# A four-tap convolution whose first tap is written by ScalarE instead of VectorE, in a one-layer hybrid decoder step

## The chip, the cores and the metric

The kernel runs on one core of a Trainium2 chip. The core has TensorE (PE in the profile; its weight loads are listed as PEld), VectorE (DVE), ScalarE (ACT), GpSimd (POOL) and SyncE (SP, which here only issues DMAs). Each engine works through its own instructions strictly in the order of its queue. The metric is the device time of one execution in microseconds (us).

## What is computed

One step of a decoder layer with three parallel branches: differential attention, a Mamba-2 state space branch (SSD) and a gated delta rule branch (GDN). One input projection feeds all of them. The columns of the projection that go to the SSD (1024) and to the GDN (1536) pass through a causal convolution of four taps per channel before their SiLU; the query, key, value and gate columns do not.

```python
proj = jnp.dot(h, w['in'])                     # 1024 prompt rows, 8 sample rows

def causal_conv(x, buf, w):                    # CONV_W = 4
    L = x.shape[1]
    xp = jnp.concatenate([buf.astype(x.dtype), x], axis=1)
    y = xp[:, 0:L] * w[0]
    for i in range(1, CONV_W):
        y = y + xp[:, i:i + L] * w[i]
    return y, xp[:, L:]

xbc, conv1 = causal_conv(xbc, conv0, conv_w)   # SSD: silu(xbc + conv_b)
qkv, conv1 = causal_conv(qkv, conv0, conv_w)   # GDN: silu(qkv)
```

## The kernel before

The input projection is computed feature-major. An item is 128 output columns (channels, on the partitions); there are 44 items: 4 query, 4 key, 4 value, 12 gate (`z_item`), 8 SSD convolution (`x_item`) and 12 GDN convolution (`g_item`) items. `proj_fm` takes the items in a fixed list. An item is three blocks of 344 token columns, n = 0, 1, 2. A block is 24 matmuls (8 slices of the contraction, times three products of high and low halves of the operands, line 458) into one PSUM bank of the ring `pj`, which has three banks; so the matmuls of a block can't begin before the bank of the block three places earlier has been read out. When a block is done, the item's `sink` reads the bank. Query, key, value and gate items are read by one ScalarE copy per block (lines 563, 577, 600, 990). Convolution items are read by `conv_item`'s sink on VectorE: one `tensor_scalar_mul` with the factor of the last tap (line 964), and then three `scalar_tensor_tensor` instructions (helper `stt`, line 167) that read the bank shifted by one to three columns and add onto `y` (tile `cy`, 128 x 1024 in SBUF). After the third block the item's `tail` columns are copied (line 971), and `silu_flush` runs SiLU over whole `cy` tiles on ScalarE, with loads of the activation table when the function changes (lines 155, 186). The convolution has 20 items, so 60 blocks, 60 first taps and 180 further taps.

ScalarE also splits the weights of the next item: `w_split` writes the high half (`whi`, line 155 through `act`), and GpSimd the low half (`wlo`, line 201). There are three buffers for half an item's weights.

Other streams run beside the projection. `gdn_head` inverts a triangular matrix of each GDN head: its blocks go from tile `LT` to DRAM (`invd`, line 1126) and come back as `Dm` (line 1129); VectorE does 31 elimination steps of two instructions on tile `U` with `Dm` (lines 1141 and 1142, helper `tt` at line 159); `U` goes to DRAM (line 1146) and comes back into `LT` (line 1149); then TensorE transposes it (line 1158), and the head's recurrence follows. All four of these DMAs are issued from ScalarE's queue, so what stands behind one of them there waits until its condition holds. `sample_attention` streams cache pages: GpSimd multiplies key pages (`kt`, line 840), VectorE reduces them to `lg` (line 841), TensorE multiplies value pages (`vt`, line 886).

The order on each engine is laid down when the kernel is built: a scheduler places the instructions of all streams by its own estimate of when they can run, with the priorities that `drive` and `boost` give. On the chip the queues then run in that order.

Of the kernel before, what the change touches and what calls it, by code (L numbers as in the profile page):

```python
# [13 lines left out]
AF = mybir.ActivationFunctionType  # L14
# [73 lines left out]
def trunk_kernel(  # L88
# [9 lines left out]
    V, S, G, TE, SP = nc.vector, nc.scalar, nc.gpsimd, nc.tensor, nc.sync  # L98
# [37 lines left out]
    def unit(shape, dt=F32, n="u"):  # L136
        return up.tile(shape, dt, tag="u", name=nm(n))
# [15 lines left out]
    def act(out, in_, func, bias=0.0, scale=1.0, accum=None):  # L153
        if accum is None:
            return S.activation(out, in_, func, bias=bias, scale=scale)  # L155
        return S.activation(out, in_, func, bias=bias, scale=scale, accum_out=accum)  # L156
# [9 lines left out]
    def stt(out, a, s, b, op0, op1):  # L166
        return V.scalar_tensor_tensor(out=out, in0=a, scalar=s, in1=b, op0=op0, op1=op1)  # L167
# [777 lines left out]
    def silu_flush():  # L945
        for y, bias, done in late_silu:
            i = act(y, y, AF.Silu, bias=bias)
        exp_ln_tables(i)
        for y, bias, done in late_silu:
            done(y)  # L950
        late_silu.clear()

    def conv_item(c0, wb, ws, ti, tj, done, flush, silu_bias=0.0):
        wv = [vec[:, wb + i * ws + ti:wb + i * ws + ti + 1] for i in range(4)]
        cur = [None]

        def sink(n, ps):
            if n == 0:
                cur[0] = unit([P, T], n="cy")
            y = cur[0]  # L960
            o = 3 if n else 0
            m = CH if n < 2 else CH - NS
            c0_ = n * CH
            V.tensor_scalar_mul(y[:, c0_:c0_ + m], ps[:, o:o + m], wv[3])
            for i in range(3):
                s_ = 0 if n else 3 - i
                q = o - 3 + i + s_
                yv = y[:, c0_ + s_:c0_ + m]
                stt(yv, ps[:, q:q + m - s_], wv[i], yv, ALU.mult, ALU.add)
            if n == 2:  # L970
                V.tensor_copy(tail[:, tj, :], ps[:, o + m - 3:o + m + NS])
                late_silu.append((y, silu_bias, done))
                if flush:
                    silu_flush()

        return (c0, sink, 3)
# [623 lines left out]
    def pages_of(f):  # L1600
        return take(smp, f * S_ALL), f * S_ALL
# [89 lines left out]
    for n1 in CUTS:  # L1691
# [5 lines left out]
        ps = pages_of(SF[1] * f)  # L1697
# [239 lines left out]
```

## Time and profile before

| | us |
|---|---|
| median of 3 runs | 1262.76 |
| lowest, highest run | 1250.82, 1265.09 |
| the profiled execution | 1275.71 |
| its span, first to last instruction | 1274.0 |
| TensorE busy in the span | 1139.0 |
| VectorE, ScalarE, GpSimd busy | 803.8, 476.2, 641.8 |

The profiled execution took 1.7 us more than its span, and 13 us more than the median run. The projection lies between about 60 and 856 us of the span. Then come the rest of the attention, of the SSD and of the GDN, and from about 1120 us the output projection.

Busy time is the time in which an engine executes something. A row of a view in order of time has the start, the duration, the engine, the line, the operation, output<-input by the tiles' names, the shape and the number of merged instructions; in square brackets stands the idle time of the engine just before, and what ended it. PEclk is the granted clock of TensorE, as a share of its upper level.

### The profile page before, as it was taken

How to read it: one execution, taken by the hardware profiler on the slowest of the kernel's cores; microseconds unless marked ns; L12 is line 12 of the kernel's file. 1: busy time of each engine (PE TensorE's matmuls, PEld its weight loads, DVE VectorE, ACT ScalarE, POOL GpSimd, SP SyncE). 2: the span in 40 equal slices, each digit the busy share in tenths (PEclk: the TensorE clock that was granted, in tenths of full speed). 3: DMA queues.
4: the chain of work that ended last, by engine and by line, in shares of the span. 5: the costliest groups of instructions: out<-in, count | busy, mean ns of one | idle time of the engine just before them, and what ended most of it. 6: DMA issues, size and time to landing. Idle time of an engine off the chain costs nothing.

```text
span 1274.0 us, 22286 instructions
## 1 busy us (share of the span) xinstructions
PE 1139.0 (89%) x7364; PEld 956.3 (75%) x7365; DVE 803.8 (63%) x1933; ACT 476.2 (37%) x1014; POOL 641.8 (50%) x778
## 2 busy tenths in 40 slices
PE   5999998988889988989997899978898999799997
PEld 4799887777658868768876779856577778678876
DVE  6613386538658668944655924877877888664444
ACT  6332223201123532233352244345647658341111
POOL 3747964644567573473975688841032151241100
PEclk9999998988879998998998999999998999899999
DMA  8646864993796883695896799998884663961420
GB/s 297 199 164 206 275 206 126 339 317 92 233 315 202 279 278 84 219 323 182 281 338 189 220 333 319 332 266 222 243 201 126 160 172 114 297 216 54 130 69 34
DMA packets 246451, 275.56 MB, mean 216 GB/s; under 512 B 31905, under 2 KB 163376, under 8 KB 246322
## 3 DMA queue, kind: packets, MB, share of 16 engines
q1 hardware_dynamic: 168082, 214.44, 52.1%
q10 hardware_dynamic: 78256, 59.72, 16.7%
q8 instruction: 58, 0.95, 0.3%
q14 instruction: 55, 0.45, 0.1%
HBM read 231.59 MB, written 42.67 MB: 215 GB/s over the span
## 4 chain that ended last, share of the span: by engine, by line
PE 49%; DMA 18%; DVE 17%; ACT 4%; issue 4%; POOL 3%; SPq 3%; ACTq 1%; DVEq 0%; POOLq 0%
PE b L458 20%; PE b L1826 10%; DVE U L159 4%; DMA vt<-in_cache_v_dram 4%; PE pv L886 3%; DMA kt<-in_cache_k_dram 2%; DMA w<-in_w_in_dram 2%; POOL kt L840 2%; DVE lg L841 2%; DVE cy L167 2%; SPq L821 1%; PE b L745 1%; DMA sbc<-bcd 1%; DVE e L721 1%; DMA Dm<-invd 1%
## 5 line engine op out<-in xcount | busy, mean ns | idle before, releaser
L458 PE MATMUL b<-hh,whi 128*128 128x344 f32 (+1 forms) x2016 | 504.6, 333 | 25.5 <-DVE cy L167 13.9
L840 POOL TENSOR_TENSOR kt<-kt,qb 128x256 f32<-128x256 f32 x512 | 364.1, 747 | 137.8 <-DMA kt<-in_cache_k_dram 82.4
L458 PEld LDWEIGHTS b<-hh,whi 128*128 128x128 f32 x2016 | 358.0, 194 | 57.1 <-issue 30.3
L458 PE MATMUL b<-hh,wlo 128*128 128x344 f32 (+1 forms) x1008 | 329.1, 331 | 3.4 <-POOL wlo L201 3.3
L841 DVE TENSOR_REDUCE lg<-kt 128x16 f32<-128x1024 f32 x128 | 154.8, 1212 | 101.8 <-POOL kt L840 94.7
L458 PEld LDWEIGHTS b<-hh,wlo 128*128 128x128 f32 x1008 | 194.5, 194 | 16.2 <-issue 10.9
L201 POOL TENSOR_TENSOR wlo<-w,whi 128x512 fp32r<-128x512 f32 x86 | 111.0, 1295 | 96.7 <-ACT whi L155 95.4
L1826 PE MATMUL b<-wo,mh 128*128 128x512 f32 (+1 forms) x408 | 121.8, 380 | 0.0
L155 ACT ACTIVATE whi<-w 128x512 fp32r<-128x512 f32 x86 | 53.8, 630 | 141.2 <-PE b L458 86.2
L167 DVE SCALAR_TENSOR_TENSOR cy<-b,vec,cy 128x341 f32<-128x341 f32 (+4 forms) x180 | 98.9, 564 | 1.5
L886 PE MATMUL pv<-vt,wz 128*32 128x512 f32 x512 | 78.8, 631 | 16.2 <-DMA vt<-in_cache_v_dram 12.7
L1826 PEld LDWEIGHTS b<-wo,mh 128*128 128x128 f32 x408 | 74.7, 188 | 14.1
L1826 PE MATMUL b<-wo,ml 128*128 128x512 f32 (+1 forms) x204 | 77.2, 378 | 0.0
L1794 POOL TENSOR_TENSOR ml<-zt,mh 128x512 fp32r<-128x512 f32 x16 | 22.4, 1401 | 104.6 <-ACT mh L1793 89.5
L155 ACT ACT_TABLE_LOAD x36 | 46.2, 1283 | 30.4 <-DMA qh<-qfd 11.0
L159 DVE TENSOR_TENSOR U<-U,Dm 128x60 f32<-128x60 f32 (+24 forms) x124 | 42.3, 341 | 16.7 <-DMA Dm<-invd 14.7
L156 ACT ACTIVATE e<-e,nmx 128x128 f32<-128x128 f32 (+7 forms) x64 | 49.1, 768 | 8.5 <-issue 5.2
L718 PE MATMUL b<-kTh,qh 128*128 128x128 f32 (+3 forms) x96 | 40.9, 433 | 9.4 <-DVE mx L721 7.2
L159 DVE TENSOR_TENSOR U<-U 128x60 f32<-128x60 f32 (+24 forms) x124 | 44.4, 358 | 2.4
L159 DVE TENSOR_TENSOR y<-b,gate 128x512 f32<-128x512 f32 (+1 forms) x17 | 11.1, 659 | 53.6 <-PE b L1826 53.6
L721 DVE CUSTOM_DVE_ANT_0 e<-b,bt 128x512 f32<-128x512 f32 (+3 forms) x64 | 36.9, 581 | 12.0 <-PE b L719 9.9
L1826 PEld LDWEIGHTS b<-wo,ml 128*128 128x128 f32 x204 | 38.4, 188 | 7.3
(524 smaller groups left out, 1964.0 us busy)
## 6 DMA issues: line engine op xcount, KB each, us to landing
kt<-in_cache_k_dram SPq DMA_DIRECT2D x256, 256.0 KB
vt<-in_cache_v_dram SPq DMA_DIRECT2D x256, 256.0 KB
w<-in_w_in_dram ACTq DMA_DIRECT2D x82, 256.0 KB
zfd<-zf ACTq DMA_DIRECT2D x12, 512.0 KB
wo<-in_w_out_dram SPq DMA_DIRECT2D x12, 512.0 KB
om<-mixd SPq DMA_DIRECT2D x24, 256.0 KB
xt<-in_x_prompt_dram SPq DMA_DIRECT2D x8, 512.0 KB
hx<-in_w_ada_dram SPq DMA_DIRECT2D x16, 256.0 KB
```

The costliest lines, as they stand in the source:

```text
L155: return S.activation(out, in_, func, bias=bias, scale=scale)
L156: return S.activation(out, in_, func, bias=bias, scale=scale, accum_out=accum)
L159: return V.tensor_tensor(out=out, in0=a, in1=b, op=op)
L167: return V.scalar_tensor_tensor(out=out, in0=a, scalar=s, in1=b, op0=op0, op1=op1)
L201: G.tensor_tensor(out=lo, in0=w32, in1=hi.bitcast(F32), op=ALU.subtract)
L458: TE.matmul(ps[:, 0:N], a, b[k][:, sl], start=(i == 0), stop=(i == 23))
L718: TE.matmul(ps[:, 0:b - a], qh[:, m, ts], kT[m][:, a:b], start=True, stop=False)
L721: V.tensor_tensor_reduce(out=e[m][:, a:b], in0=ps[:, 0:b - a], in1=bias, scale=1.0, scalar=-3.0e38, op0=ALU.add, op1=ALU.max, accum_out=mx ...
L840: G.tensor_tensor(out=kt[:, j, c], in0=kt[:, j, c], in1=qb[:, c], op=ALU.mult)
L841: V.tensor_reduce(out=lg[:, 2 * g:2 * g + 2, :], in_=kt.rearrange("p j (a d) -> p j a d", d=64), axis=AX.X, op=ALU.add)
L886: mm = TE.matmul(pv[32 * r:32 * r + 32, :], wz[:, 2 * g + j, :], vt[:, j, :], start=(b == 0 and g < 2), stop=(b == NS - 1 and g >= 14 and ...
L1826: TE.matmul(ps[c], m[a][:, kt % 4, :], w[kt][:, c[0]:c[1]], start=(kt == KT[0] and i == 0), stop=(kt == KT[-1] and i == 2))
```

## The change

One line of `conv_item`'s sink: the first tap of a convolution block is no longer a VectorE multiplication but a ScalarE activation `Copy` whose scale is the same per-channel factor. The three further taps, the copy of the tail and all else stay in the code as they were.

```diff
             m = CH if n < 2 else CH - NS
             c0_ = n * CH
-            V.tensor_scalar_mul(y[:, c0_:c0_ + m], ps[:, o:o + m], wv[3])
+            act(y[:, c0_:c0_ + m], ps[:, o:o + m], AF.Copy, scale=wv[3])
             for i in range(3):
                 s_ = 0 if n else 3 - i
```

Sixty instructions leave VectorE's queue and sixty stand on ScalarE's. Since the scheduler places all streams anew, other instructions change their places too, on all engines; ScalarE's queue has 58 table loads where it had 53.

The first place is VectorE in the elimination steps of the first GDN head. `cy_3400` is a convolution item and `b_3375` the bank of its first block. Before:

```order
L159 TENSOR_TENSOR U_2827<-U_2827,Dm_2822 128x65
L964 TENSOR_SCALAR cy_3400<-b_3375,vec 128x344
L159 TENSOR_TENSOR U_2827<-U_2827 128x5x13
L159 TENSOR_TENSOR kb_3417<-kN_2484,f_340_2569 128x1024
L167 SCALAR_TENSOR_TENSOR cy_3400<-b_3375,vec,cy_3400 128x341
L159 TENSOR_TENSOR U_2827<-U_2827,Dm_2822 128x60
L159 TENSOR_TENSOR lg_2030<-lg_2030,b_3182 128x264
L167 SCALAR_TENSOR_TENSOR cy_3400<-b_3375,vec,cy_3400 128x342
L159 TENSOR_TENSOR U_2827<-U_2827 128x5x12
L964 TENSOR_SCALAR cy_3400<-b_3428,vec 128x344
L167 SCALAR_TENSOR_TENSOR cy_3400<-b_3375,vec,cy_3400 128x343
```

After the change, on the same engine:

```order
L159 TENSOR_TENSOR U_2827<-U_2827,Dm_2822 128x76
L159 TENSOR_TENSOR kb_3417<-kN_2484,f_340_2569 128x1024
L159 TENSOR_TENSOR U_2827<-U_2827 128x4x19
L167 SCALAR_TENSOR_TENSOR cy_3400<-b_3375,vec,cy_3400 128x341
L159 TENSOR_TENSOR U_2827<-U_2827,Dm_2822 128x72
L167 SCALAR_TENSOR_TENSOR cy_3400<-b_3375,vec,cy_3400 128x342
L159 TENSOR_TENSOR U_2827<-U_2827 128x4x18
L167 SCALAR_TENSOR_TENSOR cy_3400<-b_3375,vec,cy_3400 128x343
L159 TENSOR_TENSOR U_2827<-U_2827,Dm_2822 128x68
```

The three taps that empty bank `b_3375` now stand some nine elimination steps earlier (the steps count down from 128x76 over 128x72 and 128x75 to 128x60).

The second place is ScalarE at the end of the elimination of the second GDN head (`U_5170`). `cy_5812` is a convolution item, `cy_6109` the next one (with banks `b_6084` and then `b_6149`). Before:

```order
L155 ACTIVATE whi_5949<-w_734_5785 128x512
L155 ACTIVATE whi_6114<-w_764_6080 128x512
L194 DMA w_765_6082<-in_w_in_dram 128x4x128
L155 ACTIVATE cy_5812<-cy_5812,vec 128x1024
L186 ACT_TABLE_LOAD
L194 DMA w_786_6267<-in_w_in_dram 128x4x128
L1146 DMA invd<-U_5170 256x1x32 x4
L1582 DMA yxd<-cy_5812 128x1024
L1149 DMA LT_4934<-invd 32x8x32 x4
L155 ACTIVATE whi_6178<-w_765_6082 128x512
```

After:

```order
L155 ACTIVATE whi_5949<-w_734_5785 128x512
L1146 DMA invd<-U_5170 256x1x32 x4
L155 ACTIVATE cy_5812<-b_5985,vec 128x336
L194 DMA w_765_6082<-in_w_in_dram 128x4x128
L155 ACTIVATE whi_6114<-w_764_6080 128x512
L1149 DMA LT_4934<-invd 32x8x32 x4
L155 ACTIVATE cy_5812<-cy_5812,vec 128x1024
L186 ACT_TABLE_LOAD
L155 ACTIVATE cy_6109<-b_6084,vec 128x344
L194 DMA w_786_6267<-in_w_in_dram 128x4x128
L1582 DMA yxd<-cy_5812 128x1024
L155 ACTIVATE cy_6109<-b_6149,vec 128x344
```

The first taps of three blocks now stand behind the store of `U` (line 1146) or behind the load that waits for that store to land (line 1149), where before no read-out of a bank stood. On TensorE, the transposes of this head (line 1158) have moved too: they stood inside block `b_6271`, the first block of the item behind `cy_6109`, with 15 of its 24 matmuls and 12 of the next block ahead of them; now they stand inside block `b_6202`, the last block of `cy_6109`, with eight of its matmuls behind them.

## Rows read from the trace of the kernel before

**Rows 1.** Stretch, length; busy (count) of PE, PEld, DVE, ACT, POOL; PEclk, DMA, GB/s.
```profile
60.00:856.00 796.00, 720.92 (x4663) 615.82 (x4661) 483.54 (x974) 249.12 (x430) 517.95 (x649) 0.95 0.76 244
```

**Rows 2.** The page: busy time by engine; the chain that ended last, by engine.
```profile
PE 1139.0 (89%) x7364; PEld 956.3 (75%) x7365; DVE 803.8 (63%) x1933; ACT 476.2 (37%) x1014; POOL 641.8 (50%) x778
...
PE 49%; DMA 18%; DVE 17%; ACT 4%; issue 4%; POOL 3%; SPq 3%; ACTq 1%; DVEq 0%; POOLq 0%
```

**Rows 3.** The chain between 60 and 856 us, shares by line.
```profile
by line: PE b L458 31.5%; DVE U L159 6.7%; DMA vt<-in_cache_v_dram 4.8%; PE pv L886 4.3%; issue 4.2%; DMA kt<-in_cache_k_dram 3.5%; POOL kt L840 3.0%; DVE lg L841 2.9%; DVE cy L167 2.9%; DMA w<-in_w_in_dram 2.5%; SPq L821 1.8%; DMA sbc<-bcd
```

**Rows 4.** Groups by shape: count, busy us, mean ns, idle us before, releasers.
```profile
L155 ACT ACT_TABLE_LOAD x36 | 46.2, 1283 | 30.4 <-DMA qh<-qfd 11.0 <-DMA vt<-in_cache_v_dram 4.8 <-DMA LT<-invd 3.5
...
L964 DVE TENSOR_SCALAR cy<-b,vec 128x344 f32<-128x344 f32 x40 | 22.4, 567 | 3.8 <-PE b L458 3.8
...
L155 ACT ACTIVATE em<-b,bs 128x256 f32<-128x256 f32 x32 | 13.5, 473 | 24.6 <-PE b L1110 17.1 <-DMA vt<-in_cache_v_dram 4.8 <-PE b L458 2.6
...
L964 DVE TENSOR_SCALAR cy<-b,vec 128x336 f32<-128x336 f32 x20 | 11.1, 555 | 7.0 <-PE b L458 7.0
...
L990 ACT COPY zf<-b 128x344 f32<-128x344 f32 x24 | 10.4, 447 | 49.1 <-PE b L458 21.3 <-DMA invd<-U 10.8 <-DMA vt<-in_cache_v_dram 8.0
L155 ACT ACTIVATE oC<-b,f 128x128 f32<-128x128 f32 x28 | 10.2, 364 | 50.7 <-DVE vn L159 42.2 <-DVE lg L841 6.4 <-POOL wlo L201 2.2
```

**Rows 5.** Line 167 on the convolution's tile: count, shortest/median/longest ns, first and last start.
```profile
L167 DVE SCALAR_TENSOR_TENSOR cy<-b,vec,cy x180: 546/565/577, 163.0 to 850.1; 128x344 f32<-128x344 f32 x60, 128x336 f32<-128x336 f32 x60, 128x341 f32<-128x341 f32 x20, 128x342 f32<-128x342 f32 x20
```

**Rows 6.** TensorE's waits, 160 to 856 us: us in total, times, longest.
```profile
PE b L458 <- DVE cy L167: 13.9, 8, 5.3
...
PE b L458 <- ACT zf L990: 5.8, 1, 5.8
...
PE b L608 <- ACT vT L600: 5.2, 1, 5.2
PE b L458 <- DVE tail L971: 4.3, 1, 4.3
```

**Rows 7.** VectorE in order of time, first head's elimination.
```profile
295.06 1.22 DVE L159 TENSOR_TENSOR U<-U,Dm 128x72 f32<-128x72 f32 x1
...
302.25 0.57 DVE L964 TENSOR_SCALAR cy<-b,vec 128x344 f32<-128x344 f32 x1
...
307.77 0.56 DVE L167 SCALAR_TENSOR_TENSOR cy<-b,vec,cy 128x343 f32<-128x343 f32 x1
...
327.91 0.56 DVE L964 TENSOR_SCALAR cy<-b,vec 128x336 f32<-128x336 f32 x1
...
332.14 0.67 DVE L159 TENSOR_TENSOR U<-U 128x8 f32<-128x8 f32 x1
```

**Rows 8.** TensorE in order of time, the stalls at 308 and 344 us.
```profile
308.48 0.91 PE L458 MATMUL b<-hh,whi 128*128 128x344 f32 x2 [4.27 <-DVE cy L167]
...
344.50 1.94 PE L1158 MATMUL b<-ident,LT 128*128 128x128 f32 x8 [5.61 <-DMA LT<-invd]
```

**Rows 9.** The stretches before and behind the stall's end at 308 us (columns as Rows 1).
```profile
303.00:308.40 5.40, 1.21 (x6) 0.14 (x4) 5.40 (x9) 0.94 (x2) 3.94 (x3) 0.93 0.00 1
308.40:314.40 6.00, 5.92 (x23) 5.95 (x24) 4.86 (x13) 1.28 (x1) 0.45 (x1) 0.50 0.33 88
```

**Rows 10.** VectorE in order of time: the wait that stands ahead of 480.8 us.
```profile
480.12 0.19 DVE L159 TENSOR_TENSOR U<-U,Dm 128x31 f32<-128x31 f32 x1 [2.06 <-DMA Dm<-invd]
480.23 1.53 DVE L167 SCALAR_TENSOR_TENSOR cy<-b,vec,cy 128x343 f32<-128x343 f32 x3
```

**Rows 11.** VectorE in order of time, a long instruction at 192 us.
```profile
192.12 7.08 DVE L159 TENSOR_TENSOR lg<-lg,fb 128x8 f32<-128x8 f32 x1
```

**Rows 12.** GpSimd in order of time, at 192 us.
```profile
192.26 6.92 POOL L840 TENSOR_TENSOR kt<-kt,qb 128x256 f32<-128x256 f32 x10
```

**Rows 13.** ScalarE's queue in order of time, end of the second head's elimination.
```profile
529.25 0.60 ACTq L1146 DMA_DIRECT2D invd<-U  x1
...
536.02 3.01 ACTq L1149 DMA_DIRECT2D LT<-invd  x4
```

## The prediction

> **What bounds the kernel now.** I first read the busy time by stretch. Between 60 and 856 us, where the projection and all 60 convolution blocks lie, TensorE is busy for 720.9 of 796 us, VectorE for 483.5, ScalarE for 249.1, and the granted clock is 0.95 [rows 1]. So TensorE bounds the stage, and VectorE has 39% of it free. The chain of work that ended last says the same with a hint added: over the span TensorE holds 49% of it, VectorE 17%, ScalarE 4% [rows 2]; inside the stage 31.5% is the projection's matmuls, 6.7% the elimination steps on `U`, and 2.9% the further taps of the convolution [rows 3]. The reader should see that VectorE matters only where a matmul waits for it. TensorE's waits in the stage name those places: eight waits for a tap of line 167, 13.9 us together, the longest 5.3, and one of 4.3 us for the copy of the tail [rows 6]. That is 18.2 us in nine waits, out of 60 read-outs. The rest of TensorE's lost time waits for something else (pages from the cache, ScalarE's copies, `LT`), which this edit does not remove.
>
> **What is removed.** Sixty multiplications leave VectorE, 22.4 + 11.1 = 33.5 us [rows 4]. Most of this lies beside TensorE's work. To price what doesn't, I use the further taps as a stand-in, since they stand next to the first ones and serve the same banks: they hold 2.9% of 796 us, 23.1 us of the chain [rows 3], and 180 of them at a median of 0.565 us are 101.7 us of work [rows 5]. So 0.227 of a tap's time counts, and 33.5 x 0.227 = **-7.6 us**. The bounds are 0 (the waits are made by what stands around the taps, not by the taps) and -18.2 (every wait for the read-out goes).
>
> **What is added.** ScalarE gets sixty activations with a per-partition factor. No such instruction on 344 columns of a bank is in the trace. From below it is bounded by the gate items' copy of the same shape without a factor, 447 ns; two activations from a bank with a vector operand give 364 ns for 128 columns and 473 for 256, that is 0.85 ns a column, and, drawn on to 344 columns, an estimate of 548 ns [rows 4]. I take the latter, because of the operand: 60 blocks make 32.7 us (the 336-column ones are 7 ns shorter). The upper bound is a VectorE tap, 567 ns [rows 4], so this price is not the doubt. Five more table loads at 1.283 us [rows 4] are 6.4 us. Together ScalarE has 39.1 us more. It has 4% of the chain, 51 of 1274 us, for 476.2 us of work [rows 2], so 0.107 of its time counts: **+4.2 us**. The bounds are 0 (ScalarE is busy for only 249 of the 796 us) and, by the rival on ScalarE below, some +21.
>
> The Trainium skill, "ScalarE: Activation LUTs", section "What ACT_TABLE_LOAD costs", puts a drain of about 1.38 us on top of each load's 1.28. The trace agrees with the load and has no row for a drain. By the page the five loads would be 13.3 us instead of 6.4, which at 0.107 is 0.7 us more in the sum, too little to alter it.
>
> The further taps now need ScalarE's result instead of VectorE's own. A hand-over between engines takes the place of one in order, but a matmul waits for the last tap of a bank three places back, and a block of 24 matmuls at 720.9/4663 = 0.155 us [rows 1] is 3.7 us. Two whole blocks, 7.4 us, stand between a finished bank and its next use; that covers 0.55 + 3 x 0.565 = 2.2 us and any hand-over. I cost it at nothing. The cover is gone only where VectorE or ScalarE is behind by over 5 us, and these are the places below.
>
> **The first head, 295 to 345 us.** VectorE works here without a break (5.40 of 5.40 us), while TensorE does 1.21 [rows 9]. The first tap of `b_3375` starts at 302.25 and its last at 307.77 [rows 7], because elimination steps, `kb` and `lg` stand between them (the order rows of before). TensorE waits 4.27 us for it [rows 8] and then runs for 6.0 us at a granted clock of 0.50, its lower level of 1.2 GHz, busy for 5.92 [rows 9]; at the upper level this would be about 3.0 us less. So the stall is worth 7.3 us. In the new order the three taps end before the step on 128x68, while the 128x72 step was reached at 295.06 [rows 7]. This wait should go. But the gain is not kept whole: TensorE soon comes to the transposes of line 1158, where it already waits 5.61 us for `LT` [rows 8], and `LT` can't be loaded before the elimination ends at 332.14 [rows 7]. If TensorE is 7 us earlier, it waits 7 us longer, except by what the elimination gains. Six first taps stand between 295 and 332 us on VectorE (two of them in rows 7); at 0.567 they are 3.4 us. I take **-3 us**, between 0 and -7.3.
>
> **The second head, 529 to 550 us.** ScalarE's queue issues the store of `U` at 529.25 and the load into `LT` at 536.02 [rows 13]. Between them it waits for the store to land. After the change three first taps stand behind one or both of these. With the 7.4 us of cover above, a hold of 536.02 - 529.25 = 6.8 us is just hidden when the bank was not late before. What is new is on TensorE: the transposes of line 1158 stand 8 + 15 + 12 = 35 matmuls earlier, about 5.4 us at 0.155, and the DMA they need is no earlier. In the trace of before only the first head's transposes waited long, so here there was room, of a size that no row gives. A full loss is 5.4 us plus 3.0 at the half clock; none is lost if there was as much room. I take **+5 us**, since the nearest row, the first head, waits 5.6 us.
>
> **Unchanged places.** At 480 us VectorE's wait of 2.06 us for `Dm` comes first and three further taps queue behind it [rows 10]; they still do, and only the first tap leaves. At 192 us a small `lg` addition takes 7.08 us [rows 11] while GpSimd multiplies key pages for 6.92 [rows 12]; a last tap stands behind it in both orders. I cost both at nothing; whoever removes them gets the faster rival.
>
> **Sum.** -7.6 + 4.2 - 3 + 5 = -1.4 us, on a span of 1274.0 and an execution of 1275.71. That execution lies 13 us above the median, 1262.76, whose runs reach from 1250.82 to 1265.09. Set on the median: **1261 us**. A change of under 1%, 12.6 us, is about what a measurement of this kernel can't tell from none.
>
> **Rival A, faster.** VectorE's relief breaks the long read-out waits. Three of 5.3, 4.3 and 4.3 us [rows 6] go, each with 3.0 us of half clock behind it as at 308: 13.9 + 9.0 = 22.9, less 4.2 on ScalarE, is -18.7: **1244 us**. For it speaks that these waits stand where VectorE is full; against it that two of the places keep their cause, and that the first head passes its gain on to `LT`. Chance 0.24.
>
> **Rival B, slower.** ScalarE holds the banks. Its queue issues DMAs that wait, as rows 13 show, so a first tap behind one is late by microseconds, and the three further taps then hold up VectorE's queue, elimination steps included. The 48 blocks that ScalarE alone reads now (12 value, 36 gate) had waits of 5.8 and 5.2 us [rows 6]; with 3.0 each at the half clock they are 17 us, 0.354 a block. On 60 more blocks that is 21 us: 21 - 7.6 + 4.2 = +17.6, **1280 us**. It decides from two such new stalls on, where they exceed the 12.6 us. Against it: 36 + 12 = 48 blocks had only two of them, and ScalarE is free for two thirds of the stage. Chance 0.24.
>
> **Rival C, no relief.** VectorE isn't late because of its taps, but because of GpSimd and of the DMAs for `Dm`. For it speaks the 7.08 us that an addition on 128 x 8 takes exactly while GpSimd runs [rows 11, 12], and that the taps themselves never take over 577 ns [rows 5]. Then the first term is 0, the first head's gain too, and 4.2 + 5 = +9.2 is left: **1272 us**. Chance 0.14.
> The Trainium skill, "SBUF — State Buffer", section "Who interferes with whom", says that VectorE and GpSimd share a pair of SBUF ports under an exclusive lock. The trace agrees: the `lg` addition, with two SBUF inputs, was held, and the taps, with a bank as one of theirs, were not. By that rule the edit takes away instructions that never waited on it.
>
> **How the numbers follow.** The forecast, 1261, has 0.38; its own range, with the doubts of the four terms (about 7, 3, 4 and 4 us) added as squares, is 1252 to 1270. Forecast and rival C lie within 1%: same 0.52. Rival A is faster, 0.24, rival B slower, 0.24. If some four tenths of A and of B are left out at the ends, the range is 1241 to 1282.
>
> **What would show it.** VectorE's busy time should fall by about 33 us and ScalarE's rise by about 39, with activations on the bank of some 0.55 us. The wait of 4.27 us at 308 should be gone, with the wait for `LT` there longer, and the second head's transposes should wait some 5 us. TensorE's waits for VectorE's taps should sum to about 10 us instead of 18. I am wrong if the waits for taps fall under 5 us and none replaces them (A), or if taps whose first one hung behind a DMA issue of ScalarE stall TensorE twice or more (B), or if taps wait in the same places as before (C). A new stall in a place that moved with the order, far from any tap, would be a cause that none of these names.

## The result

The changed kernel is faster: 1247.3 us as the median of 20 runs, against 1265.64 for 20 runs of the kernel before, a ratio of 0.9885 with a 95% interval of 0.9865 to 0.9905. That is 14.5 us of 1264. (The ratio leaves disturbed runs out, so it is nearer to 1 than that of the two medians, 0.9855.) The prediction said 1261, with a range of 1241 to 1282. The time lies inside the range, 14 us below the point, next to the 1244 of the faster rival. The two profiled executions differ by more, 31 us of span (1274.0 and 1242.8), because the one of before is longer (1275.71) than any of its 20 timed runs (at most 1274.01). So differences between the two traces are used here for places, and the timed ratios for sizes.

The page of the changed kernel, busy time by engine and the chain that ended last; before in [rows 2]:

```profile
PE 1139.0 (92%) x7364; PEld 953.9 (77%) x7365; DVE 755.8 (61%) x1873; ACT 511.2 (41%) x1079; POOL 643.9 (52%) x778
...
PE 55%; DMA 16%; DVE 10%; ACT 7%; POOL 4%; issue 3%; SPq 2%; ACTq 2%; DVEq 0%; POOLq 0%
```

VectorE lost 48 us and ScalarE gained 35. The sixty taps are 33.5 us of the 48; VectorE has just 60 instructions fewer, so the rest is instructions that took less time. VectorE's share of the chain fell from 17% to 10%, which is far more than sixty taps. Next the groups of the new instructions by shape, with count, busy time and mean ns; the estimate was 548 and 541 ns from [rows 4]:

```profile
L155 ACT ACTIVATE cy<-b,vec 128x344 f32<-128x344 f32 x40 | 21.3, 547 | 52.5 <-PE b L458 39.2 <-POOL kt L840 6.5 <-issue 5.5
...
L155 ACT ACTIVATE cy<-b,vec 128x336 f32<-128x336 f32 x20 | 10.6, 532 | 16.3 <-DMA invd<-U 6.3 <-PE pv L886 3.9 <-POOL kt L840 3.5
```

TensorE's waits in the stage, 160 to 856 us, in us, times and longest; before in [rows 6]:

```profile
PE b L458 <- ACT zf L990: 5.7, 1, 5.7
...
PE b L458 <- DVE cy L167: 3.7, 3, 2.7
...
PE b L1158 <- DMA LT<-invd: 2.1, 2, 1.1
```

The waits for VectorE's read-out fell from 18.2 us to 3.7, those for `LT` from 5.6 to 2.1, and none for a first tap on ScalarE is among the longer ones. At the first head, where TensorE stood until 308.48 and again until 344.50 [rows 8], it now works without a break at the upper clock level. These are two windows of the changed kernel, with the columns of [rows 1]:

```profile
292.00:300.00 8.00, 8.00 (x55) 6.95 (x53) 8.00 (x25) 1.93 (x4) 4.19 (x5) 1.00 0.78 220
300.00:308.00 8.00, 8.00 (x49) 6.95 (x48) 6.82 (x16) 1.06 (x2) 4.12 (x5) 1.00 1.02 333
```

The last elimination step of the first head on VectorE:

```profile
303.21 0.16 DVE L159 TENSOR_TENSOR U<-U 128x8 f32<-128x8 f32 x1
```

And the head's transposes on TensorE:

```profile
315.62 1.06 PE L1158 MATMUL b<-ident,LT 128*128 128x128 f32 x8 [1.04 <-DMA LT<-invd]
```

The elimination ends at 303 us, where it ended at 332 [rows 7]. Followed by the ends of line 458's matmuls, 24 (a block) at a time, TensorE's lead over the trace of before is 12 us at the end of the 28th block of the projection, 24 us at the 49th (315 us here, 339 before), and 26 us at the 127th, the last. So most of the 31 us is won in the first 340 us.

### The profile page after: what moved, and what is told of

Same layout as the page of the kernel before. It is cut to its first block, busy times and chain, and to the rows that moved or that the text cites. A ratio compares the mean times of both kernels' runs of the same rounds, so it can differ in the third digit from the quotient of the medians.

```text
span 1242.8 us, 22286 instructions
## 1 busy us (share of the span) xinstructions
PE 1139.0 (92%) x7364; PEld 953.9 (77%) x7365; DVE 755.8 (61%) x1873; ACT 511.2 (41%) x1079; POOL 643.9 (52%) x778
## 4 chain that ended last, share of the span: by engine, by line
PE 55%; DMA 16%; DVE 10%; ACT 7%; POOL 4%; issue 3%; SPq 2%; ACTq 2%; DVEq 0%; POOLq 0%
PE b L458 25%; PE b L1826 9%; PE pv L886 4%; DMA w<-in_w_in_dram 3%; DMA vt<-in_cache_v_dram 2%; DVE U L159 2%; POOL kt L840 2%; DMA kt<-in_cache_k_dram 1%; DVE lg L841 1%; ACT e L156 1%; DMA hx<-in_w_ada_dram 1%; PE b L745 1%; ACT wo L155 1%; POOL wlo L201 1%; PE b L1886 1%
## 5 line engine op out<-in xcount | busy, mean ns | idle before, releaser
L167 DVE SCALAR_TENSOR_TENSOR cy<-b,vec,cy 128x341 f32<-128x341 f32 (+3 forms) x180 | 99.7, 566 | 30.8 <-ACT cy L155 29.6
L886 PE MATMUL pv<-vt,wz 128*32 128x512 f32 x512 | 85.3, 639 | 8.4 <-issue 5.2
L155 ACT ACTIVATE cy<-b,vec 128x344 f32<-128x344 f32 (+1 forms) x60 | 31.7, 542 | 68.8 <-PE b L458 41.7
L745 PE MATMUL b<-vh,wT 128*128 128x128 f32 x288 | 41.3, 290 | 3.5 <-ACT wT L738 3.3
```

The lines of the kernel that those rows point to most:

```text
L745: TE.matmul(po[:, 0:P], wTs[j // 4][:, j % 4, :], vh[:, j, :], start=(j == 0), stop=(j == i))
L886: mm = TE.matmul(pv[32 * r:32 * r + 32, :], wz[:, 2 * g + j, :], vt[:, j, :], start=(b == 0 and g < 2), stop=(b == NS - 1 and g >= 14 and ...
```

## The experiments

There are two things in the change: sixty instructions go to another engine, and the scheduler places everything anew. To take them apart, a kernel was given the order of another one: behind the program's construction, each engine's instructions are chained in a listed order (issue order only, no waits).

```diff
     with _tile.TileContext(nc, schedule_with_timeline_sim=True) as tc:
         trunk_kernel(tc, *args)
+        _hold_order(tc)
```
```python
    traced = {i.name: i for i in tc.nc.cur_bb.bb.instructions}
...
            if prev is not None:
                tc.add_manual_dep(i, prev, _m.DependencyInfo(_m.DependencyClass.NoSync, _m.DependencyReason.DATA),
                                  reason="hold_order")
            prev = i.name
```

The theories: **1**, the engine (VectorE is relieved where it is full); **2**, the order; **3**, ScalarE holds the banks; **4**, the waits only move on. The times of before in the same sessions lie between 1263.3 and 1264.8 us in the median.

### First taps on ScalarE in the old order

The diff is that of the change, with the order of before held. 

> The 60 first taps on ScalarE, but all five engines keep the order of the kernel before: ScalarE's queue gets each tap at the place where the scheduler of before had it on VectorE. Theory 1, the engine: the gain comes from VectorE's relief where it is full (the waits at 190 to 210, 265 to 285 and 308 us), so most of the 1.15% is here too: a ratio of 0.988 to 0.994, and TensorE's waits for VectorE's taps fall from 18 us to under 9. Theory 2, the order: the gain comes from the other places that all streams got when the scheduler planned anew; then this one is 0.997 to 1.003 and the waits for the read-out stay in their places. Theory 3, ScalarE holds the banks in an order that was not planned for it: over 1.005, with new waits of TensorE for taps whose first one was late.

Measured: 1266.35 us, ratio 1.0006 (0.9970 to 1.0041). Theory 1 would have had at most 0.994, so in the old order the change is worth nothing that can be measured. TensorE's waits for VectorE's read-out did fall as theory 1 said, from 18.2 us to 7.1, and the time did not follow. Theory 3 falls too. One wait is put down to a first tap on ScalarE (waits of TensorE, 160 to 856 us):

```profile
PE b L458 <- DVE cy L167: 7.1, 5, 5.8
...
PE b L458 <- ACT cy L155: 3.4, 1, 3.4
```

It ends at 302.95 us, and it is the wait of 308 us in its place: the last further tap of the first block there ended on VectorE at 302.80, 0.04 us ahead of that first tap.

### First taps on VectorE in the new order

> The order of the changed kernel on all engines, but the 60 first taps run on VectorE again, each at the place that the scheduler gave it on ScalarE. Theory 1, the engine: the relief is gone, so 0.997 to 1.006, and long waits for VectorE's taps come back. Theory 2, the order: 0.986 to 0.992, like the changed kernel. Both in equal parts: about 0.994.

> The changed kernel's order with the first taps on VectorE, once more. It had 0.9953. If the order is only half of the gain and ScalarE's taps are the other half, it is 0.993 to 0.998 and over 0.4% slower than the changed kernel beside it. If the order is the whole gain, it is within 0.3% of it.

Measured: 1255.27 us, ratio 0.9953 (0.9920 to 0.9986); once more, 1256.52 us, 0.9920 (0.9888 to 0.9952). The mean, 0.9937, is a gain of 8 us with VectorE doing all that it did before. The changed kernel beside the second one:

> The changed kernel once more, as the measure for the three others on the same chip. 0.986 to 0.991 by every theory.

It had 1245.94 us, 0.9889 (0.9835 to 0.9942). The kernel with VectorE's taps was 0.3% slower beside it, between the two expectations (over 0.4%, within 0.3%), so this pair decides little by itself. By both runs, 0.5% and 0.8% of the 1.15% are the order alone, and the rest, 0.3 to 0.7%, comes only with ScalarE's taps in that order. The intervals of the second part overlap, so its size is less certain than that of the whole.

### No first taps at all, in either order

```diff
-            V.tensor_scalar_mul(y[:, c0_:c0_ + m], ps[:, o:o + m], wv[3])
+            V.tensor_scalar_mul(y[:, c0_:c0_ + 3], ps[:, o:o + 3], wv[3])
...
-                stt(yv, ps[:, q:q + m - s_], wv[i], yv, ALU.mult, ALU.add)
+                stt(yv, ps[:, q:q + m - s_], wv[i], yv, ALU.mult, ALU.add) if i else V.tensor_scalar_mul(yv, ps[:, q:q + m - s_], wv[i])
```

> The order of the kernel before, and nothing new on ScalarE: the convolution leaves out its last factor (the first tap is only 3 columns wide, and the first of the further taps writes instead of adding), so that about 30 us of VectorE's 33.5 us of first taps are gone. It gives the price of VectorE's share alone. Theory 1: as fast as the kernel with ScalarE's taps in the old order or some 4 us faster (ScalarE's share), 0.984 to 0.992. Theory 2: 0.997 to 1.002.

> The changed kernel's order on all engines, and neither VectorE nor ScalarE does the first taps: as in the old order's kernel without them, the convolution leaves out its last factor (the first tap is 3 columns wide, and the first of the further taps writes instead of adding). With the taps on VectorE this order had 0.9953 and 0.9920, with ScalarE 0.9885 and 0.9889. If VectorE's relief is what the second half of the gain is (the elimination of the first two heads is 2 to 4 us shorter in the traces): 0.985 to 0.990. If the relief is worth nothing here either, as in the old order (1.0003), and the half came from something in ScalarE's queue: 0.992 to 0.996.

Measured: 1.0003 (0.9971 to 1.0036) in the old order, 0.9877 (0.9834 to 0.9921) in the new one. Together with the others:

| first taps | on VectorE | left out | on ScalarE |
|---|---|---|---|
| old order | 1 | 1.0003 | 1.0006 |
| new order | 0.9953, 0.9920 | 0.9877 | 0.9885, 0.9889 |

Leaving the taps out is worth no more than giving them to ScalarE, in both rows: ScalarE does them for nothing within the intervals. And VectorE's 30 us less are worth nothing that can be measured in the old order and some 4 to 9 us in the new one. Why nothing in the old order is seen in two places. The first is the read-out wait at the first head, 4.27 us before [rows 8]. Without any first taps in the old order, 3.55 us of it are still there, since the elimination steps and `kb` still stand among the further taps:

```profile
299.38 0.91 PE L458 MATMUL b<-hh,whi 128*128 128x344 f32 x2 [3.55 <-DVE cy L167]
```

The second is the wait of 480 us. This is the old order without first taps, VectorE in order of time; before in [rows 10]:

```profile
466.31 1.52 DVE L969 TENSOR_SCALAR cy<-b,vec 128x341 f32<-128x341 f32 x3
467.75 1.52 DVE L167 SCALAR_TENSOR_TENSOR cy<-b,vec,cy 128x342 f32<-128x342 f32 x3
471.51 0.19 DVE L159 TENSOR_TENSOR U<-U,Dm 128x31 f32<-128x31 f32 x1 [2.24 <-DMA Dm<-invd]
471.62 1.53 DVE L167 SCALAR_TENSOR_TENSOR cy<-b,vec,cy 128x343 f32<-128x343 f32 x3
```

The matmul of the same kernel that waits for these taps:

```profile
472.24 0.94 PE L458 MATMUL b<-hh,whi 128*128 128x344 f32 x2 [5.11 <-DVE cy L167]
```

VectorE idles for 2.24 us ahead of `U`, and the last three taps stand behind it. What VectorE saves ahead of it only makes this idle time longer. TensorE's wait is 5.11 us, where it was 5.3. In the changed order it is 2.70 us at this place:

```profile
452.84 0.55 PE L458 MATMUL b<-hh,whi 128*128 128x344 f32 x2 [2.70 <-DVE cy L167]
```

### A new plan without any change of work

```diff
-GF = .77
+GF = .771
```

> The kernel before with the weight of one stream in the interleaving changed from 0.77 to 0.771: the same instructions on the same engines, about as many of them in new places as by the change studied here. Theory 1: within 0.4% of before, so that 1.15% is more than a new plan does. Theory 2: a new plan alone can move the time by 1% to either side.

Measured: 1281.41 us, ratio 1.0147 (1.0105 to 1.0189). A plan of the same instructions on the same engines can be 1.5% slower. A change whose gain is 1.15% is no larger than what this new plan does by itself, and the prediction had no term for that. Which of the places makes this plan slower was not taken apart.

### Two waits mended by hand in the old order

On VectorE, the four taps of `b_3375` are put ahead of the step on 128x75, and the first step of the second head behind the taps of 480 us; nothing else moves.

> The kernel before with VectorE's first taps and the old order on all engines, but for two places on VectorE: the four taps of b_3375 stand ahead of the elimination step on 128x75 (they end near 297 us and not at 308), and the last three taps of the item at 480 us, with the copy of its tail, stand ahead of the first elimination step of the second head, which waits for Dm. Theory 2 (order: the read-out waits come from what stands ahead of the taps, not from the taps' time): both waits, 4.3 and 5.3 us, shrink to under 1 and to under 3, and with 3.0 us of half clock behind each some 8 to 14 us are gained, less what the first head passes on to LT: a ratio of 0.990 to 0.996. Theory 4 (the waits only move on, to LT and to Dm): 0.998 to 1.002.

Measured: 1263.49 us, ratio 0.9983 (0.9947 to 1.0019), the size that theory 4 expected; a small gain is not excluded. In its trace the wait at 308 us is gone and the one at 480 us is shorter. But a wait for `sm` comes up in the first one's place, and other waits stay (TensorE's waits, 160 to 856 us, and the new wait in order of time):

```profile
PE b L458 <- DVE cy L167: 7.2, 6, 3.0
...
PE b L1158 <- DMA LT<-invd: 4.5, 1, 4.5
PE b L458 <- DVE tail L971: 4.4, 1, 4.4
...
PE b L608 <- ACT vT L600: 4.1, 1, 4.1
```
```profile
299.46 0.38 PE L854 MATMUL b<-ident,sm 8*128 8x8 f32 x2 [2.50 <-DVE sm L853]
```

The wait for `LT` did not grow, as theory 4 would have it; it is 4.5 us, where it was 5.61.

### Which part of the order

> ScalarE's first taps, with the changed kernel's order up to the last matmul of the 49th projection block (about 315 to 340 us), and the order of the kernel before from there on. In the two traces the lead of the changed kernel grows to some 24 us by that point and hardly after it, but 7 us of it is one wait at 200 us that other runs of the old order lack. If the early part is where the order pays: 0.989 to 0.993. If the later sites (480 us) have the same share: 0.994 to 0.997. If the order of the early part is worth nothing alone: 0.999 to 1.002.

Measured: 1248.74 us, ratio 0.9883 (0.9842 to 0.9924). The order up to 315 us of the changed kernel gives the whole gain, and the later places give nothing measurable. This includes the second head, which the prediction priced at 5 us, and the wait at 480 us: with the old order there, the trace of this kernel has a longest wait of 5.4 us for a tap, as before.

> First taps on VectorE, the order of the kernel before on all engines, but VectorE follows the changed kernel's order up to the end of the 49th projection block. If the gain comes from the elimination of the first head, whose 62 steps take 50 to 54 us in the old order and 40 to 42 in the new one because fewer other instructions stand between them on VectorE: the steps take under 44 us and the ratio is 0.990 to 0.994. If VectorE's order is worth nothing without the others': 0.998 to 1.004.

> The same with ScalarE alone in the changed kernel's order up to there. If the gain comes from ScalarE's queue (the value copies that stand behind the load of Dm, TensorE's wait of 5.2 us near 270): that wait goes and the ratio is 0.993 to 0.997; by the theory of the elimination 0.998 to 1.002, with 50 to 54 us for the 62 steps.

> The same with TensorE alone in the changed kernel's order up to there. If the gain comes from where TensorE's own work stands (the head's products earlier among the projection's matmuls): the head's store into DRAM, which starts at 246 to 254 us in the old order and at 242 to 248 in the new one, comes earlier by 4 to 10 us and the ratio is 0.991 to 0.996; by the theory of the elimination 0.998 to 1.003.

Measured: VectorE alone in the new early order 1.0051 (1.0020 to 1.0083), ScalarE alone 0.9999 (0.9971 to 1.0028), TensorE alone 1.0114 (1.0086 to 1.0142). None gives the gain, and two lose. TensorE alone met neither expectation: the head's store into DRAM (line 1126) starts at 257.52 us in its trace, 3 us later than before (254.52). With VectorE alone in it, ScalarE in the old order waits for what VectorE now does later: the transposes wait 8.55 us for `LT` and not 5.61, because ScalarE's store of `U` stands behind a SiLU that gets its input later. ScalarE and its queue in order of time, with the elimination's end at 330.7 us ahead of it:

```profile
334.03 1.06 ACT L155 ACTIVATE cy<-cy 128x1024 f32<-128x1024 f32 x1 [8.75 <-DVE cy L167]
334.03 3.43 ACTq L1146 DMA_DIRECT2D invd<-U  x4
```

And the transposes of that kernel on TensorE:

```profile
347.69 1.94 PE L1158 MATMUL b<-ident,LT 128*128 128x128 f32 x8 [8.55 <-DMA LT<-invd]
```

The elimination took 49 us there (281.5 to 330.7), and not the 39 to 43 of the new order as a whole, though as many other instructions (41) stand between its steps on VectorE as there. So VectorE's own order does not make it short, and whether a short elimination carries the gain is left open by this run.

### What differs in the early part

The traces show some things that go with the new early order. That these make up the gain is argued from the traces, since no run took them apart. TensorE's longer waits between 160 and 360 us, in us:

| order, first taps | read-out, first head | `vT` (line 600) | `LT` |
|---|---|---|---|
| old, VectorE (before) | 4.3 | 5.2 | 5.6 |
| old, left out | 3.5 | 4.7 | 5.2 |
| old, ScalarE | 3.4 | 5.1 | 3.5 |
| new, VectorE | at most 0.3 | 1.0 | 2.1 |
| new, ScalarE | at most 0.3 | 0.7 | 1.0 |

All three waits stay in the old order, whoever does the taps, and shrink in the new one. The prediction had a term for the first, let the third grow, and had none for the second.

The elimination of the first head is shorter in the traces of the new order. These are its 31 products by `Dm` on VectorE (shortest, median and longest ns, first and last start) in the kernel before:

```profile
L159 DVE TENSOR_TENSOR U<-U,Dm x31: 165/230/1650, 278.9 to 331.5; 128x60 f32<-128x60 f32 x3, 128x28 f32<-128x28 f32 x2, 128x54 f32<-128x54 f32 x2, 128x48 f32<-128x48 f32 x2
```

In the old order without first taps:

```profile
L159 DVE TENSOR_TENSOR U<-U,Dm x31: 166/218/1648, 270.6 to 321.5; 128x60 f32<-128x60 f32 x3, 128x28 f32<-128x28 f32 x2, 128x54 f32<-128x54 f32 x2, 128x48 f32<-128x48 f32 x2
```

In the new order with the taps on VectorE:

```profile
L159 DVE TENSOR_TENSOR U<-U,Dm x31: 168/220/1517, 263.9 to 305.6; 128x60 f32<-128x60 f32 x3, 128x28 f32<-128x28 f32 x2, 128x54 f32<-128x54 f32 x2, 128x48 f32<-128x48 f32 x2
```

In the changed kernel:

```profile
L159 DVE TENSOR_TENSOR U<-U,Dm x31: 174/221/1516, 264.0 to 301.5; 128x60 f32<-128x60 f32 x3, 128x28 f32<-128x28 f32 x2, 128x54 f32<-128x54 f32 x2, 128x48 f32<-128x48 f32 x2
```

From the first to the last start these are 52.6, 50.9, 41.7 and 37.5 us. Taking out sixty first taps shortens it by 1.7 us in the old order; the new order shortens it by 11, with all taps on VectorE.

Over half of the 11 us is in the steps themselves. These are the stretches of the 62 steps, before and in the new order with the taps on VectorE: length, busy (count) of VectorE and of GpSimd on `U`, PEclk, DMA, GB/s.

```profile
278.90:332.90 54.00, 26.40 (x62) 0.00 (x0) 0.94 0.53 167
```
```profile
263.80:306.50 42.70, 20.34 (x62) 0.00 (x0) 1.00 0.64 198
```

The same steps take 6 us less. Counted in the two traces, a step that starts while GpSimd executes an instruction takes 0.66 and 0.53 us in the median, and no other step takes over 0.24. Before, 26 of the 62 steps meet GpSimd like this; in the new order 18. In the kernel before, a run of GpSimd's products, a step inside it and the step behind its end at 301.71 us:

```profile
296.15 5.56 POOL L840 TENSOR_TENSOR kt<-kt,qb 128x256 f32<-128x256 f32 x8
```
```profile
301.14 0.66 DVE L159 TENSOR_TENSOR U<-U,Dm 128x70 f32<-128x70 f32 x1
301.84 0.23 DVE L159 TENSOR_TENSOR U<-U 128x70 f32<-128x70 f32 x1
```

GpSimd's order is another one too: in this part its product on `kN` (line 1152) stood behind a run of eight products and stands behind four now. No run gave GpSimd alone, or the DMA queue of SyncE alone, the new early order, so what these contribute is not shown.

In the second head taking the first taps out does more: it makes 48.7 us (480.1 to 528.8) into 45.1 (471.5 to 516.6) in the old order, but the total time does not show it.

Last, the small `lg` addition of [rows 11] is not held through GpSimd's ten products. It took 7.08 us before and in the kernel with the two moves, and 7.07 us in the other plan. In the old order without first taps, VectorE in order of time:

```profile
191.64 0.87 DVE L159 TENSOR_TENSOR lg<-lg,fb 128x8 f32<-128x8 f32 x1
```

GpSimd in that kernel, a split of weights and the run of products:

```profile
191.20 1.28 POOL L201 TENSOR_TENSOR wlo<-w,whi 128x512 fp32r<-128x512 f32 x1
192.44 7.01 POOL L840 TENSOR_TENSOR kt<-kt,qb 128x256 f32<-128x256 f32 x10
```

The addition in the changed kernel:

```profile
186.59 0.17 DVE L159 TENSOR_TENSOR lg<-lg,fb 128x8 f32<-128x8 f32 x1
```

And the products there:

```profile
187.94 7.01 POOL L840 TENSOR_TENSOR kt<-kt,qb 128x256 f32<-128x256 f32 x10
```

Before, a first tap stands right ahead of the addition, and GpSimd's ten products begin 0.14 us after the addition's start (192.26 against 192.12, [rows 11, 12]), directly behind a split that was already running then:

```profile
191.02 1.29 POOL L201 TENSOR_TENSOR wlo<-w,whi 128x512 fp32r<-128x512 f32 x1
```

Without that tap's length (the tap of 3 columns takes 0.21 us, not 0.58) the addition starts earlier in the split and ends with it, after 0.87 us, ahead of the products. With ScalarE's taps in the old order it took 1.01 us and ended with the split as well. So here a first tap itself can make a wait: TensorE stood 4.3 us for the copy of the tail behind the addition [rows 6]. The tap alone does not decide it: with ScalarE alone in the new order, a tap of 0.57 us stands ahead of the addition too, and it took 0.53 us. And the old-order kernels that escape the long hold are no faster than before in their timed runs. Either the lead is given back, or the timed runs of before are held there less often than the profiled one; no run shows which.

## Why the prediction came out as it did

**The sum was small, and the change is not.** Range and direction held (-0.1% forecast, -1.15% measured), but the point was too cautious by some 14 us, and the terms were right only in part. By the signs that the prediction itself gave, it was wrong: the waits for taps fell to 3.7 us, under the 5 that it had named as a sign for rival A, VectorE's busy time fell by 48 us and not by 33, and the wait for `LT` became shorter, not longer. That the time lies in the range is owed to the room that was left in it for rival A, and not to the mechanism.

**VectorE's relief, -7.6 us.** The step was to let each first tap count like a further tap on the chain, 0.227 of its time. In the old order it counted 0 (1.0003, the interval being about 4 us to either side), in the new order some 4 to 9 us. The share of a line on the chain is not a price of that line: taps stood on the chain because they queue behind a wait for `Dm` or behind elimination steps, and shorter taps only wait longer. The bound of 0, and rival C's reasoning, were right for the order that the trace showed.

**ScalarE's load, +4.2 us.** Measured about +1 us in the new order (0.9887 in the mean of two against 0.9877 with no taps at all) and 0 in the old one, within the intervals. The duration was right, 547 ns for 548. The chain's share as a price failed here as well.

**The first head, -3 us.** This is the step that failed most. The place was right: the wait of 4.27 us went, as the order rows said. But I held the rest of the elimination fixed except for six first taps, 3.4 us, and so let TensorE wait for `LT` 7 us longer. It began 15 us earlier and was 14 us shorter, so that it ended 29 us earlier, in one profile against the other, and the wait for `LT` fell from 5.61 us to 1.04. Part of this is steps that no longer meet GpSimd, and I had no term for that. (The taps of `b_3375` moved by six elimination steps of two instructions, not by nine; nothing in the sum hangs on it.) The order up to there is worth the whole 14.5 us with ScalarE's taps (0.9883). I had read two places of the order and priced two places; the gain lies in the orders of the engines from 185 to 315 us taken together; neither VectorE's, ScalarE's nor TensorE's alone gives it, and what within them does it stays open. The kernel with the two moves shows what mending places alone gives: one wait went, the other fell from 5.3 to 3.0 us, and nothing over 0.5% came of it.

**The second head, +5 us.** No new wait of that size: the two waits for `LT` in the changed kernel sum to 2.1 us. The elimination there is shorter by 6 us too, which is about what the earlier place of the transposes takes (5.4). First taps did stand behind the store of `U`; the one that waited 6.31 us for it is in the second group shown above (by its releaser), and TensorE did not wait for it, as the 7.4 us of cover said.

**Unchanged places.** Costing 192 and 480 us at nothing was wrong for the trace and harmless for the sum: both waits shrank, and the run with the changed order in its early part alone shows that the later one is not worth anything measurable.

**The rivals.** A, the faster one, named the right time (1244) by the wrong mechanism: the long read-out waits do go, but with the taps still on VectorE too (5.7 us of waits in the new order). With the taps away in the old order they fall as well, to 7.1 and 9.9 us, and no time is gained. So that A's time was near was luck. B would have shown as a loss in the old order with ScalarE's taps; there was none. C is right about the relief in the old order, but not about its 9 us of loss. That a new plan may move the time by over 1% by itself, to either side, was no rival of mine and should have been one, with the many rows that the order moves, on all engines, as its ground.

The Trainium skill, "SBUF — State Buffer", section "Who interferes with whom", has VectorE and GpSimd share ports under an exclusive lock. The trace agrees with it: the addition with two SBUF inputs took 7.08 us when it met GpSimd's products and 0.14 to 1.09 us when it ended ahead of them, the elimination steps took 0.66 us beside GpSimd and 0.23 behind it, and the further taps, with a bank as an input, stayed at about 0.56 us. I weighed the rule for the taps alone, as a ground against the change, and passed over the elimination steps, which take longer beside GpSimd too and which a new plan places anew.

## What to carry to other kernels

When a scheduler places all streams anew, test first what a new plan of the same work does to the time (here 1.0147), and hold the old order while moving the work, before giving the gain to the engine that was relieved. The share that a line has on the chain tells where the end is set, not what the line's removal is worth: look at what the instructions queue behind, and whether the engine idles just before them. Two waits mended alone gave nothing that could be measured; a gain came only where several engines had the new order together.

## What was not expected of the hardware

An addition on 128 x 8 took between 0.14 and 1.09 us, or 2.76, 4.35 or 7.08 us in different kernels, by when it met GpSimd's run of ten products; half a microsecond earlier saved six. This addition is held to the end of the run and not to the end of one product: with TensorE alone in the new order it started inside the run, at 196.18 us, and ended 2.76 us later, at 198.94, where the run ends too (192.02 + 6.90 = 198.92). The elimination steps are not: inside the run of eight shown above (5.56 us, 0.70 a product) one step after the other got through, at 0.66 us each. No run shows why the two differ. Executions of one kernel spread by up to 1.9% (1250.82 to 1274.01 for the 20 of before), so a single profile can show a difference of 31 us where the medians show 18.
